# Softmax over rows of 512: one load of 32 rows in place of two of 16, and one reciprocal moved ahead of one maximum

## The chip, the cores and the metric

The kernel runs on one core of a Trainium2 chip. The core has several engines, each with its own stream of instructions. Three of them compute here: VectorE (DVE in the profile), ScalarE (ACT) and GpSimd (POOL). A fourth, SyncE (SP), only issues transfers between the chip's DRAM and the core's on-chip memory; the transfers themselves are carried by 16 DMA engines. TensorE is not used. Engines wait for one another through semaphores.

The metric is the time of one execution on the device in microseconds (us). Before the change it is 159.53 us, the median of three runs that lie between 159.28 and 159.63. A difference of less than 0.2% (0.32 us) can hardly be told from no change.

## The reference

```python
x: (16, 1024, 512) float32
x_max = np.max(x, axis=-1, keepdims=True)
exp_x = np.exp(x - x_max)
return exp_x / np.sum(exp_x, axis=-1, keepdims=True)
```

It is a softmax along the last axis of 16,384 rows of 512 numbers: 33.55 MB are read and 33.55 MB are written.

## The kernel before, in words

The 16,384 rows are spread over the 128 partitions of the on-chip memory, 128 rows to a partition, and below "row 40" means the 40th row of every partition. Rows are transferred in blocks and computed in groups of 8. So there are 16 groups: rows 0 to 7 are group 0, rows 32 to 39 are group 4, rows 120 to 127 are group 15.

**Transfers.** `BLOCKS` (line 21) cuts the 128 rows into blocks. Inside a block each partition's rows are neighbours in DRAM, so a block of 16 rows is one piece of 32 KB for each partition, and a block of 32 rows one of 64 KB (`in_dram`). `ORDER` (line 22) lists loads ("L") and stores ("S") in the order in which SP issues them. Before, it is: loads of rows 0-15, 16-31, 32-47, 48-63, 64-95; then stores of 0-15, 16-31, 32-47; loads of 96-111 and 112-127; stores of 48-63, 64-95, 96-111, 112-127. A store may take half of a block, and `in_dram` then takes half of each partition's piece. The first `AHEAD` entries are issued at once, without a wait; the very first load is even moved ahead of the program's opening barrier. Every later one waits for what it needs: a store for the groups that it holds, a load into the ring of 96 rows (`held`) for the store of the rows that lay there. `AFTER` (line 41) adds waits of a chosen kind: the first store is not issued before group 4 is scaled, the loads of 96 and 112 not before groups 8 and 9 are, and the store of 48-63 not before group 11 is.

All transfers go through one hardware queue, and each of the 16 DMA engines takes its share of them one after the other.

**Work on a group.** For group g:

- M*g*, on DVE (line 168): the negated maximum of each of its rows. DVE first waits for the load that holds the group (`take(nc.vector, loaded[k], 16)`).
- ACT (line 212), in a loop over the groups: for each row, the exponential with the maximum as bias, with its sum as a second result. It waits for M*g* once per group (`maxed`).
- P*g* (line 176, `scale`): DVE makes the reciprocal of the 8 sums, waiting for ACT's group g, and then POOL multiplies the rows by it (line 182). For groups 0 to 11.
- V*g*: the same with the multiplication on DVE. For groups 12 to 15.

DVE works through one list that is written out by hand, `VECTOR` (line 45). DVE takes it strictly in order: an entry that waits holds up all that are behind it. POOL takes its groups in order too, and each multiplication waits for its own reciprocal.

Of the kernel before, what the change touches and what calls it, by code (L numbers as in the profile page):

```python
# [17 lines left out]

BLOCKS = [(0, 16), (16, 32), (32, 48), (48, 64), (64, 96), (96, 112), (112, 128)]
ORDER = [
    ("L", (0, 16)),
    ("L", (16, 32)),
    ("L", (32, 48)),
    ("L", (48, 64)),
    ("L", (64, 96)),
    ("S", (0, 16)),
    ("S", (16, 32)),
# [5 lines left out]
    ("S", (96, 112)),  # L35
    ("S", (112, 128)),
]
AHEAD = 5

# [2 lines left out]


VECTOR = """
    M0 M1 P0 M2 P1 M3 P2 M4 P3 M5 P4 M6 P5 M7 P6 M8 P7 M9 P8 M10 P9 M11
    P10 P11 M12 M13 V12 M14 V13 M15 V14 V15
"""

# [24 lines left out]
def kernel(  # L75
# [13 lines left out]
    def in_dram(rows, a, b):  # L89

        first, last = next(k for k in BLOCKS if k[0] <= a and b <= k[1])
        block = rows[first * P : last * P].rearrange("(p r) d -> p r d", p=P)
# [34 lines left out]
    def load(k):  # L127
        copy = nc.sync.dma_start(out=rows(*k), in_=in_dram(x_rows, *k))
        copy.then_inc(loaded[k], 16)
        return copy  # L130
# [4 lines left out]
    with tc.manual_schedule():  # L135
        for _, k in ORDER[:AHEAD]:
            tc.no_tile_sem_insts.add(load(k).ins.name)
# [3 lines left out]
    taken, done = set(), set()  # L141
    for what, k in ORDER[AHEAD:]:
        for g in range(GROUPS):
# [112 lines left out]
```

## Time and profile before

| what | value |
|---|---|
| median of three runs | 159.53 us |
| the profiled execution's own time | 159.34 us |
| its span, first to last instruction | 158.0 us |
| DMA: 67.11 MB in 14 transfers | mean 425 GB/s |
| POOL, 12 multiplications | 83.7 us busy, 7018 ns each |
| DVE, 16 maxima | 70.2 us busy, 4398 ns each |
| ACT, 128 exponentials | 90.4 us busy, 707 ns each |
| DVE, 16 reciprocals | 3.2 us busy, 201 ns each |

The profile is of one execution; times in it are counted from the span's start. The 1.3 us between the span and the execution's own time lie before and after the instructions. "DVEq L112" and the like is an engine's queue that waits in `take` (line 112) for a semaphore. A DMA packet is what one DMA engine moves at a time: 32 KB (one partition's piece of 16 rows), 64 KB (of 32 rows), or the 4 bytes with which each engine reports at the end of a transfer; the transfer has landed when all 16 have reported.

From the trace's records, the five loads at the head landed in full at 12.28, 21.98, 31.68, 41.41 and 60.76 us.

### The profile page before, as it was taken

Reading aid. Unit: us, or ns where it says so; the run is one execution under the profiler, and the core shown is the slowest. Engines: PE = TensorE matmul, PEld = TensorE weight load, DVE = VectorE, ACT = ScalarE, POOL = GpSimd, SP = SyncE. Lnnn points to the kernel's source line nnn. Section 1 sums busy time; section 2 is a strip of 40 time slices with the busy share of each in tenths; the row PEclk is TensorE's granted clock in tenths of the full one; section 3 lists DMA queues with packets and bytes.
Section 4 is the critical chain, followed back from the end, with each engine's and each line's share of the span. In section 5 each row is a group of like instructions: output and inputs, shape, how many; then the busy total and the mean of one; then the engine's idle time right before and its main releaser. Section 6 shows DMA issues by size and latency. Waiting matters only on the chain. (4 is left out here: it accounts for less than half of the span.)

```text
span 158.0 us, 716 instructions
## 1 busy us (share of the span) xinstructions
DVE 90.0 (57%) x36; ACT 92.1 (58%) x257; POOL 83.9 (53%) x16
## 2 busy tenths in 40 slices
DVE  0008959778877915969770000695999996920000
ACT  1100699999999998399999300049946839000000
POOL 0000009999999999999999999991000000000000
DMA  8999999999969979999999999999999969999996
GB/s 265 423 481 423 398 456 465 406 415 481 564 265 531 481 315 398 423 481 423 398 448 465 406 406 398 415 498 415 398 448 481 531 265 531 390 406 406 465 456 265
DMA packets 2016, 67.11 MB, mean 425 GB/s; under 512 B 224, under 2 KB 224, under 8 KB 224
## 3 DMA queue, kind: packets, MB, share of 16 engines
q1 hardware_dynamic: 2016, 67.11, 99.1%
HBM read 33.55 MB, written 33.55 MB: 425 GB/s over the span
## 5 line engine op out<-in xcount | busy, mean ns | idle before, releaser
L212 ACT ACTIVATE held<-held,shift x128 | 90.4, 707 | 39.0 <-ACTq L112 39.0
L182 POOL TENSOR_TENSOR held<-held,recip 128x4096 f32<-128x4096 f32 x12 | 83.7, 7018 | 23.1 <-POOLq L112 23.1
L168 DVE TENSOR_REDUCE shift<-held 128x8 f32<-128x4096 f32 x16 | 70.2, 4398 | 27.7 <-DVEq L112 27.7
L212 ACT ACTIVATION_READ_ACCUMULATOR held<-held,shift x128 | 23.9, 187 | 0.0
L182 DVE TENSOR_TENSOR held<-held,recip 128x4096 f32<-128x4096 f32 x4 | 17.7, 4424 | 0.1
L176 DVE RECIPROCAL recip<-sums 128x8 f32<-128x8 f32 x16 | 3.2, 201 | 21.4 <-ACT held L212 19.5
L205 ACT ACT_TABLE_LOAD x1 | 1.3, 1283 | 3.4 <-PEq L139 3.4
L240 POOL MEMSET const-float32-0.0<- 128x1 f32 x1 | 0.1, 99 | 0.2 <-issue 0.2
L240 POOL MEMSET const-bfloat16-1.0<- 128x1 bf16 x1 | 0.1, 102 | 0.0
L240 POOL MEMSET const-uint8-127<- 128x1 uint8 x1 | 0.1, 102 | 0.0
L240 POOL MEMSET const-float32-1.0<- 128x1 f32 x1 | 0.1, 99 | 0.0
## 6 DMA issues: line engine op xcount, KB each, us to landing
held<-in_x_dram SPq DMA_DIRECT2D x6, 4096.0 KB, 18.7
out_dram<-held SPq DMA_DIRECT2D x6, 4096.0 KB, 19.8
held<-in_x_dram SPq DMA_DIRECT2D x1, 58.5
out_dram<-held SPq DMA_DIRECT2D x1, 30.8
```

The lines of the kernel that those rows point to most:

```text
L168: nc.vector.reduce_max(out=stats(shift, g), in_=rows(*group(g)), axis=AX, negate=True).then_inc(maxed, 1)
L176: ratio = nc.vector.reciprocal(out=stats(recip, g), in_=stats(sums, g))
L182: product = engine.tensor_mul(out=rows(*group(g)), in0=rows(*group(g)), in1=stats(recip, g).unsqueeze(2).to_broadcast([P, GROUP, d]),)
L205: nc.scalar.preload_act_table(EXP)
L212: act = nc.scalar.activation(out=row, in_=row, func=EXP, bias=shift[:, at], scale=1.0, accum_out=sums[:, at],)
L240: nc = _bacc.Bacc("TRN2", target_bir_lowering=False, num_devices=1)
```

## The change

The blocks (32, 48) and (48, 64) become one block (32, 64), and so do their two loads, which makes the loads at the head four instead of five. In DRAM the rows of the new block are dealt to the partitions 32 at a time, as in block (64, 96). The stores of rows 32-47 and 48-63 stay two transfers; each now takes half of every partition's 64 KB. On DVE, P3 goes ahead of M4.

```diff
-BLOCKS = [(0, 16), (16, 32), (32, 48), (48, 64), (64, 96), (96, 112), (112, 128)]
+BLOCKS = [(0, 16), (16, 32), (32, 64), (64, 96), (96, 112), (112, 128)]
 ORDER = [
     ("L", (0, 16)),
     ("L", (16, 32)),
-    ("L", (32, 48)),
-    ("L", (48, 64)),
+    ("L", (32, 64)),
     ("L", (64, 96)),
     ("S", (0, 16)),
...
-AHEAD = 5
+AHEAD = 4
...
 VECTOR = """
-    M0 M1 P0 M2 P1 M3 P2 M4 P3 M5 P4 M6 P5 M7 P6 M8 P7 M9 P8 M10 P9 M11
+    M0 M1 P0 M2 P1 M3 P2 P3 M4 M5 P4 M6 P5 M7 P6 M8 P7 M9 P8 M10 P9 M11
     P10 P11 M12 M13 V12 M14 V13 M15 V14 V15
 """
```

## The prediction

> **What bounds the kernel now.** First the page's parts on busy time and on DMA queues.
>
> ```profile
> DVE 90.0 (57%) x36; ACT 92.1 (58%) x257; POOL 83.9 (53%) x16
> q1 hardware_dynamic: 2016, 67.11, 99.1%
> ```
>
> No computing engine is busy for more than 58% of the span, and the one DMA queue keeps its 16 engines busy for 99.1%. So the time is the packets of 14 transfers end to end. Computing costs something only where a transfer is issued too late and the DMA engines run dry. The question is at which hand-over from one transfer to the next that is close. All loads at the head are queued by 2.65 us, so the first candidate is the first store: in the timelines of POOL and of SP,
>
> ```profile
> 51.45 13.99 POOL L182 TENSOR_TENSOR held<-held,recip 128x4096 f32<-128x4096 f32 x2
> 58.56 0.35 SPq L155 DMA_DIRECT2D out_dram<-held  x1
> ```
>
> POOL starts group 4 at 51.45 (the row holds groups 4 and 5) and ends it 7.02 later, at 58.46; SP issues the store 0.10 after that, at 58.56. How long an issue takes to become packets is seen in the DMA view of the first 2 us (40 slices of 0.05 us, counted by the packets' starts), and how close this hand-over is in the same view of 59.4 to 60.4 us (slices of 0.025 us):
>
> ```profile
> DMA  0000000000000000000099999999000000000000
> DMA packets 16, 0.52 MB, mean 262 GB/s; under 512 B 0, under 2 KB 0, under 8 KB 0
> ...
> DMA  0000000000090000090099990900900000999000
> DMA packets 32, 0.52 MB, mean 524 GB/s; under 512 B 16, under 2 KB 16, under 8 KB 16
> ```
>
> In the first, idle engines get their first packets in slices 20 to 27: by the records 1.02 to 1.39 us after the issue at 0.00. In the second, 16 engines report the end of the last load (4 bytes) and start on the store (32 KB) in the same slices, from 59.68 to 60.31 by the records: no gap at all, but the first engine starts on the store only 1.11 us after its issue. So there is hardly any slack here. The store of 48-63, issued at 107.38, is as close: there one engine stood idle for 0.15 us and got its first packet 1.56 us after the issue. The other hand-overs have 2.4 us or more.
>
> Third, DVE's timeline, which tells when maxima and reciprocals come:
>
> ```profile
> 28.74 4.37 DVE L168 TENSOR_REDUCE shift<-held 128x8 f32<-128x4096 f32 x1
> 34.27 0.20 DVE L176 RECIPROCAL recip<-sums 128x8 f32<-128x8 f32 x1 [1.16 <-ACT held L212]
> 34.39 4.42 DVE L168 TENSOR_REDUCE shift<-held 128x8 f32<-128x4096 f32 x1
> 39.91 0.20 DVE L176 RECIPROCAL recip<-sums 128x8 f32<-128x8 f32 x1 [1.10 <-ACT held L212]
> ...
> 45.55 0.20 DVE L176 RECIPROCAL recip<-sums 128x8 f32<-128x8 f32 x1 [1.16 <-ACT held L212]
> ...
> 51.20 0.20 DVE L176 RECIPROCAL recip<-sums 128x8 f32<-128x8 f32 x1 [1.11 <-ACT held L212]
> ...
> 60.89 4.42 DVE L168 TENSOR_REDUCE shift<-held 128x8 f32<-128x4096 f32 x1 [3.85 <-DVEq L112]
> ...
> 71.44 0.20 DVE L176 RECIPROCAL recip<-sums 128x8 f32<-128x8 f32 x1 [1.74 <-ACT held L212]
> ```
>
> and in ACT's
>
> ```profile
> 65.66 0.72 ACT L212 ACTIVATE held<-held,shift  x1 [3.20 <-ACTq L112]
> ```
>
> The rows at 34.39, 39.91 and 45.55 are M4, P3 and P4. M8 (60.89) is the pattern for a group that waits for its load: landed at 60.76, M8 0.13 later, ACT on group 8 at 65.66 (4.77 after M8's start), P8 at 71.44 (5.78 after that).
>
> **The change, part by part.**
>
> *One load for two.* By the landings, two loads of 16 rows took 19.43 us (21.98 to 41.41), and the one of 32 rows 19.34 (41.41 to 60.76). So the loads end 0.09 earlier: the last engine is free for the store at 60.22 instead of 60.31, the first at 59.59. Between no gain and this 0.09 I take the row itself. The issue that SP saves (0.4 to 0.5 us near 1.6) hides behind the first load.
>
> The Trainium skill prices a transfer higher: "DMA: Bandwidth & Descriptors", section "Anatomy of one DMA", fits about 2.0 us fixed plus the bytes' time for each. By that one transfer less would give about 157.5. The rows above, 0.09 for two against one, do not bear it out while a queue holds several.
>
> *Rows 32 to 47 land later.* They came at 31.68 and now come with the whole block, at 21.98 + 19.34 = 41.32. M4 moves from 34.39 to 41.32 + 0.13 = 41.46. ACT was fed without a break through groups 3, 4 and 5 (P3, P4, P5 are 5.65 apart); now it ends group 3 at 39.9 and starts group 4 at 41.46 + 4.77 = 46.22, so it idles for 6.3 us. P4 moves from 45.55 to 46.22 + 5.78 = 52.01. Adding 0.20 for the reciprocal and 0.04 until the waiting multiplication starts (the gap in the one place where POOL's queue waits for a reciprocal), POOL has group 4 at 52.25. Before, its reciprocal was 5.7 us early; POOL was free at 51.45. So POOL now waits, for 0.80 us, ends group 4 at 59.26, and SP issues the first store at 59.36.
>
> Behind P4 on DVE stand M6, P5 and so on. M6 starts at 52.13 and ends at 56.5, before ACT ends group 5 (57.5); P5 comes at 57.65, and POOL wants it at 59.23. P6 and later have more, since ACT's groups are 5.65 apart and POOL's 6.97. M8 would come at 63.4 instead of 60.89, behind P6, P8 at 74.6, POOL wants it at 80.1. So POOL's 0.80 neither grows nor shrinks to its end.
>
> *P3 ahead of M4.* P3 needs ACT's group 3 (39.9), and M4 now can't start before 41.46: P3 keeps its 39.91, and M4 loses nothing. Without the swap P3 would stand behind M4's wait until 45.8, over 1 us late for POOL's group 3 at 44.47. Cost nil.
>
> *The stores of 32-47 and 48-63* now write 32 KB of every 64 KB. No row shows this; the transfers of 64-95 put their pieces at the same distance and run at the usual pace (2.418 us per 64 KB packet against 1.213 per 32 KB), so I take nil. The slowest transfer of 32 KB packets in the records, the load of 96-111, took 0.46 us of packet time more than its like; twice that, 0.92, is the upper bound; none speaks for a gain.
>
> *The first store, late by 0.80.* Engines are free from 59.59 to 60.22. The store's packets come at 59.36 plus 1.02 to 1.39 by the head's rows, up to 1.56 by the one store that came late: the last at 60.76 to 60.93. Before, the last engine started on it at 60.31. So all that follows is late by 0.45 to 0.62. I take 0.62, the row of the same kind of transfer in the same place in the program. Whether a store's first packet into an empty engine is longer, as the head's loads are (1.53 to 2.28 against 1.21), isn't shown: the store's packet after 0.15 idle took 1.22. I take nothing, with up to 1.06 more as the other end.
>
> *Does it come twice?* The store of 48-63 waits for POOL's group 11, now 0.80 late: issued at 108.18, its last packets come by 109.74. The engines reach it at 109.27 + 0.62 = 109.89 at the latest. So the second lateness hides in the first. Nothing is close behind it: the next store is issued 0.46 later, the last two more than 8 us early.
>
> Sum: 159.34 + 0.62 = 159.96 on the profiled execution, which lies 0.19 under the median; on the median, 159.53 + 0.62 = 160.15.
>
> **The rivals.**
>
> *The store is there in time (not slower).* If a store is turned into packets within 60.22 - 59.36 = 0.86 us, the last engine doesn't wait, and only the 0.09 is left: 159.44, no change. For it: at 59.68 the first engine had its packet 1.11 after the issue without a gap, so the true time there is only known to be at most that. Against: 16 idle engines at the head all needed 1.02 or more. 10%, and most of it is a partial effect, about 0.2.
>
> The Trainium skill gives this its number: "DMA: Bandwidth & Descriptors", section "Specifications", has about 0.6 us to the first byte for transfers issued from SP. By that the packets would be there from 59.96 and the sum be 159.44; the head's 1.02 to 1.39 disagrees.
>
> *An empty queue costs more than the wait.* If the store's first packets are stretched as the first load's were (1.95 on the mean, 0.74 more), it is 160.89; with the slower halves of the stores, up to 161.8. For it: loads do it. Against: the 1.22 us packet, and that a store reads on-chip memory. 17%.
>
> *The load is split in effect, or merging saves more.* If M4 could start on the block's first half, at about 31.7, P4 would stay where it was and 159.44 be left; but `rowmax` waits for all 16 reports, which each engine sends behind its last packet. A gain over 0.32 would need a saving by the merge three times the 0.09 of the rows, and no wait after it. 4%.
>
> The fixed cost that the Trainium skill names (above) would be such a gain.
>
> **How the numbers follow.** The forecast holds 69%, no harm 10%, the stretched restart 17%, a gain 4%. Differences under 0.2% (0.32 us) can't be told from none, and the forecast's low end of 0.45 is near that, so some of it counts as the same: slower 0.80, same 0.16, faster 0.04. The range goes from 159.7 (a partial effect) to 160.9 (the stretched restart); the forecast's own is 159.95 to 160.3.
>
> **What would show it.** M4 at 41.5, P4 at 52.0, POOL idle 0.8 before group 4, the first store issued near 59.36; a gap of 0.2 to 1.3 us on every DMA engine near 60, and the last load's end 0.09 earlier; no larger gap at 109. Wrong would be: no gap near 60 (rival one), first store packets of 1.5 us or more (rival two), 32 KB packets longer than 1.22 in the stores of 32-63, or POOL waiting for P5 or later.

## The result, and the profile after

The changed kernel takes 160.06 us (median of 16 runs, 159.78 to 160.46) against 159.46 (16 runs, 159.23 to 159.79) before: the ratio is 1.0037, with a 95% interval of 1.0029 to 1.0045. That is 0.60 us slower, where 0.62 was forecast. The profiled execution of the changed kernel took 159.79, 0.45 more than the one of before, and its span is 158.5 instead of 158.0. It is a quick one among its runs, so the terms below are made against 0.45.

The page after, the same two rows:

```profile
DVE 90.1 (57%) x36; ACT 92.1 (58%) x257; POOL 84.0 (53%) x16
q1 hardware_dynamic: 1872, 67.11, 98.8%
```

The work is the same to 0.1 us. The DMA queue, which is the bound, is busy for 98.8% of a longer span instead of 99.1%. The timelines of DVE and ACT:

```profile
34.13 0.20 DVE L175 RECIPROCAL recip<-sums 128x8 f32<-128x8 f32 x1 [1.16 <-ACT held L211]
39.76 0.20 DVE L175 RECIPROCAL recip<-sums 128x8 f32<-128x8 f32 x1 [5.43 <-ACT held L211]
41.33 8.75 DVE L167 TENSOR_REDUCE shift<-held 128x8 f32<-128x4096 f32 x2 [1.36 <-DVEq L111]
51.87 0.20 DVE L175 RECIPROCAL recip<-sums 128x8 f32<-128x8 f32 x1 [1.80 <-ACT held L211]
51.99 4.37 DVE L167 TENSOR_REDUCE shift<-held 128x8 f32<-128x4096 f32 x1
57.51 0.20 DVE L175 RECIPROCAL recip<-sums 128x8 f32<-128x8 f32 x1 [1.16 <-ACT held L211]
```

```profile
46.09 0.72 ACT L211 ACTIVATE held<-held,shift  x1 [6.36 <-ACTq L111]
```

P3 (39.76) keeps its time, 0.15 earlier, as this execution's first load landed 0.14 earlier. M4 waits for the merged load and starts at 41.33, ACT idles for 6.36 us ahead of group 4, and P4 comes at 51.87. Then POOL, SP, and the DMA view of 59.4 to 60.4 us (slices of 0.025 us):

```profile
44.33 7.02 POOL L181 TENSOR_TENSOR held<-held,recip 128x4096 f32<-128x4096 f32 x1
52.16 7.02 POOL L181 TENSOR_TENSOR held<-held,recip 128x4096 f32<-128x4096 f32 x1 [0.81 <-DVE recip L175]
```

```profile
59.27 0.88 SPq L154 DMA_DIRECT2D out_dram<-held  x2
```

```profile
DMA  0000000000000000000000000000999999900000
DMA packets 32, 0.52 MB, mean 524 GB/s; under 512 B 16, under 2 KB 16, under 8 KB 16
```

POOL is idle for 0.81 us behind group 3, the first store is issued at 59.27, and no packet of it starts before slice 28; before, most engines had gone on to the store by then. By the records, the engines end the last load between 59.70 and 60.10 and start on the store between 60.12 and 60.27. On the mean they are idle for 0.29.

What the mean engine did from there on says where the 0.45 went (packet time and idle time per engine, from the trace's records, us):

| | before | after |
|---|---|---|
| loads at the head, end of the last one | 59.99 | 59.89 |
| idle ahead of the first store | 0.01 | 0.29 |
| stores of 0-15 and 16-31 | 19.43 | 19.55 |
| store of 32-47 and load of 96-111, with gaps | 19.94 | 20.07 |
| all that follows, to the last packet's end | 58.09 | 58.11 |

The head gives 0.10, half of it a slightly earlier first load; the idle time costs 0.28, the stores 0.12, the store and load behind them 0.13. The mean engine ends at 157.82 instead of 157.36, 0.46 later, which these terms make with 0.02 for the rest. (An engine's packets overlap by a few ns, so the columns add up to slightly more than the ends.)

### The profile page after: what moved, and what is told of

It reads as the page before. It is cut to its first block, busy times and chain, and to the rows that moved or that the text cites. A ratio compares the mean times of both kernels' runs of the same rounds, so it can differ in the third digit from the quotient of the medians.

```text
span 158.5 us, 714 instructions
## 1 busy us (share of the span) xinstructions
DVE 90.1 (57%) x36; ACT 92.1 (58%) x257; POOL 84.0 (53%) x16
## 3 DMA queue, kind: packets, MB, share of 16 engines
q1 hardware_dynamic: 1872, 67.11, 98.8%
```

## The experiments

All times are medians; the kernel before, run beside them, took 159.44 to 159.50.

**The swap alone.**

```diff
 # the kernel before
-M3 P2 M4 P3 M5 P4
+M3 P2 P3 M4 M5 P4
```

> The kernel before with the order on DVE alone changed (P3 ahead of M4). M4 then starts at 40.03 instead of 34.39, ACT's group 4 near 44.8, P4 near 50.6 instead of 45.6, and POOL wants it at 51.45, 0.7 us later than it would be there. Theory (the swap alone costs nothing): POOL without a gap, the first store at 58.56, 159.46, ratio 0.999 to 1.001. The rival, that the swap is a cost of its own: P4 later than 51.2, POOL idle, over 159.7.

159.46, ratio 1.0006 (0.9997 to 1.0015): no change. In the timelines of DVE and POOL of this kernel

```profile
50.47 0.20 DVE L176 RECIPROCAL recip<-sums 128x8 f32<-128x8 f32 x1 [1.80 <-ACT held L212]
```

```profile
37.38 69.78 POOL L182 TENSOR_TENSOR held<-held,recip 128x4096 f32<-128x4096 f32 x10
```

P4 is at 50.47, five us later than before, and POOL runs through ten groups without a gap. P4 had room, and the swap uses most of it without a cost.

**The rows' new place alone.**

```diff
 # the kernel before, ORDER, AHEAD and VECTOR as they were
-BLOCKS = [..., (32, 48), (48, 64), (64, 96), ...]
+BLOCKS = [..., (32, 64), (64, 96), ...]
```

> The kernel before with the changed rows' place in DRAM alone: the block 32-63 is dealt 32 rows to a partition, but still loaded by two transfers of 16 rows, with the old order on DVE. Loads and stores of 32-47 and 48-63 then all move 32 KB of every 64 KB. Theory 1 (the place costs nothing): 159.46, ratio 0.999 to 1.001, packets of these four transfers at 1.213 to 1.222 us. Theory 2 (half pieces are dearer): 159.65 to 159.9, with packets of 1.24 to 1.26 us in the store of 32-47.

159.47, ratio 1.0002 (0.9993 to 1.0011). Loads of half pieces run at 1.213 us a packet, the store of 32-47 at 1.227 on the mean against 1.221 before. The place costs nothing that can be measured.

**The merged load without the swap.**

```diff
 # the changed kernel
-M3 P2 P3 M4 M5 P4
+M3 P2 M4 P3 M5 P4
```

> The changed kernel with the old order on VectorE: P3 behind M4. P3 then waits for the load of 32-63 with M4 and comes near 45.7, POOL's group 3 starts near 45.95 instead of 44.33 and group 4 near 52.9 instead of 52.16. The first store is issued near 60.05, 0.77 later than in the changed kernel. Theory (each us by which that store is later is a us of the time once the engines have run dry): 160.06 + 0.77 = 160.8. If the swap did nothing: 160.06.

160.78, ratio 1.0080 (1.0067 to 1.0093), 0.72 over the changed kernel. POOL's and SP's timelines:

```profile
46.05 13.99 POOL L181 TENSOR_TENSOR held<-held,recip 128x4096 f32<-128x4096 f32 x2 [1.56 <-DVE recip L175]
```

```profile
60.14 0.88 SPq L154 DMA_DIRECT2D out_dram<-held  x2
```

POOL loses 1.56 at group 3, the store is issued 0.87 later than with the swap, and the engines are idle for 1.06 on the mean. So with the merged load the swap is worth 0.7 us; it doesn't repair P4.

**P4 late, and nothing else.** The kernel before, with its two loads; on DVE M6 and a maximum of six rows of zeros, of which nobody uses the result, go ahead of P4.

```diff
-M4 P3 M5 P4 M6 P5 M7
+M4 P3 M5 M6 G6 P4 P5 M7
...
+    def delay(n):          # G6: n = 6
+        nc.vector.reduce_max(out=spent[:, :n],
+            in_=blank.unsqueeze(1).to_broadcast([P, n, d]), axis=AX)
```

> The kernel before, with its two loads of 16 rows, and on VectorE a maximum of six rows that nobody uses ahead of P4 (and M6 ahead of that), so that P4 comes at 52.05 instead of 45.55 and POOL's group 4 at 52.27, as late as in the changed kernel. Theory (P4's lateness and nothing else in the change costs time): POOL idle 0.8, the first store issued near 59.35, the DMA engines idle by 0.2 to 0.3, and the time of the changed kernel, 160.0 to 160.2. Rival (the merged load or the places of its rows carry part of it): between 159.5 and 159.9.

160.12, ratio 1.0042 (1.0029 to 1.0055): the time of the changed kernel. POOL's timeline, SP's, and the DMA view of 59.4 to 60.4 us:

```profile
52.09 7.02 POOL L192 TENSOR_TENSOR held<-held,recip 128x4096 f32<-128x4096 f32 x1 [0.69 <-DVE recip L186]
```

```profile
59.20 0.88 SPq L157 DMA_DIRECT2D out_dram<-held  x2
```

```profile
DMA  0000000000000000000000000099999909000000
```

It is nearly the same picture, without the merged load; POOL is idle for 0.69 instead of 0.81. The engines' idle time is 0.19 on the mean, the two stores take 19.54 and the store and load behind them 20.14: the terms of the table above come with it, and the mean engine ends 0.48 later than in the kernel before.

The time itself says less than it seems to. The span from the first to the last instruction is 0.46 longer than in the kernel before (means of 5 and 11 runs); another 0.25 is lost outside the span, where this kernel spends 1.58 us and the kernel before 1.34. The changed kernel spends 1.32 there, so its loss of 0.6 lies inside. Why the kernel with the added operation takes longer outside its span was not looked into. So P4's lateness is shown to make most of the loss, 0.46 of 0.6 with a lateness that is 0.1 smaller. That it makes all of it fits these runs, but their noise doesn't decide it.

**The first store 7 us late.** The kernel before, to measure what a late issue costs at this hand-over.

```diff
-AFTER = {("S", 0): 4, ...
+AFTER = {("S", 0): 5, ...
```

> The kernel before, but the first store waits for group 5, which POOL ends at 65.44: issued at 65.53, 6.97 later, with all DMA engines idle for over 6 us. This measures how long an issued store takes to become packets and whether its first packets are longer after a gap. If it takes 0.84 to 1.00 us as in the profile after: first packets at 66.4 to 66.5, on the mean 6.45 later than before, time 165.8 to 166.0. If it takes the head's 1.02 to 1.39: 166.1 to 166.4. If the packets behind a gap are dearer by the 0.010 us of the store in the profile after (1.224 against 1.214), 0.09 us more for this store. If a first packet is stretched like the head's loads, 0.7 more.

167.18, ratio 1.0482 (1.0467 to 1.0498). SP's timeline, and the DMA view of 65 to 67 us (slices of 0.05):

```profile
65.63 0.35 SPq L155 DMA_DIRECT2D out_dram<-held  x1
```

```profile
DMA  0000000000000000000000000000099990000000
```

The idle engines start on the store 0.85 to 0.99 us after its issue; the changed kernel has 0.84 to 1.00 and the run before this one 0.85 to 1.00 (one engine there starts at 1.03, straight from the last load). Its first packets take 1.23 to 1.24, not the 1.5 to 2.3 of the head's loads. The later packets of that store take 1.224 against 1.214, also as in the changed kernel, and the two stores 19.55. So behind an idle stretch the first two stores lose 0.12, however long the stretch was. The time is 1.2 to 1.4 over what this latency gave in the expectation: the last load, of 112-127, took 10.48 instead of 9.70 and the store and load of 32-47 and 96-111 took 20.43 instead of 19.94. The next transfers had been queued 9 us ahead of their turn here, which the next two runs take up.

**The first store much earlier.** In the changed kernel (first) and in the kernel before (second):

```diff
-AFTER = {("S", 0): 4, ...
+AFTER = {("S", 0): 3, ...
```

> The changed kernel, but the first store waits for group 3 instead of group 4, so that SP issues it near 51.5 us, long before the loads at the head end near 59.9. Theory 1 (the loss is the hand-over at 60 us alone: group 4 scaled 0.8 late, the store issued at 59.27 instead of 58.56, the DMA engines idle 0.29 us on the mean): no idle time at 60, and the loss is gone: 159.46 - 0.09 = 159.37, ratio to before 0.999 to 1.000. Theory 2 (the hand-over is about half of it, since the profiles differ by 0.29 - 0.10 there, and the stores with half pieces and the transfers behind them make the rest): 159.65 to 159.85, and the store of 32-47 stays at 10.0 us instead of 9.77.

> The kernel before, but the first store waits for group 3 instead of 4 and is issued near 51.5. Theory A (a transfer of the other direction that is queued long before the one in flight ends makes the last packets of that one longer, as in the run with the changed kernel and this edit, where packets that started 3 us before the switch took 0.74 us more for each engine): the last load's packets longer again, 159.45 + 0.74 = 160.2, with no gap. Theory B (that loss belongs to the merged load or to the stores of half pieces): 159.45 and the last load at 19.35.

160.39, ratio 1.0077 (1.0053 to 1.0101), and 160.25, ratio 1.0042 (1.0028 to 1.0056). Both theories of the first fell; the second run was made to find out why, and its theory A held. The stretch from the start of the last load to its end, in the kernel before and in the changed kernel with the early store (columns: stretch, its length, busy times, clock, DMA share, GB/s):

```profile
40.66:59.99 19.33, 12.96 (x6) 19.33 (x55) 19.33 (x4) 1.00 0.96 417
```

```profile
40.65:60.71 20.06, 16.41 (x6) 14.61 (x41) 19.24 (x4) 1.00 0.98 408
```

And of the kernel before with the early store, SP's and DVE's timelines:

```profile
51.48 0.82 SPq L155 DMA_DIRECT2D out_dram<-held  x2
```

```profile
61.78 4.42 DVE L168 TENSOR_REDUCE shift<-held 128x8 f32<-128x4096 f32 x1 [4.86 <-DVEq L112]
```

The stores sit in the queue from 51.5 on, no engine is idle, and yet the last load is slower: M8 starts at 61.78 instead of 60.89. By the records the packets that started between 57 and 58 us, the last of this load on each engine, took on the mean 0.74 (first) and 1.01 us (second) more than others of their size, and hardly any other packet of the load did. A store queued 1.1 us ahead of the switch, as before, costs nothing of the kind. `AFTER`'s wait for group 4 is thus worth 0.7 to 0.8 us, and issuing the store much earlier is no cure.

**The first store in time, by another gate.** The changed kernel, and the kernel with P4 late alone. The first store now waits for a small DVE operation:

```diff
-M6 P5 M7            (changed kernel)
+M6 P5 G1 M7
-M7 P6 M8            (P4 late alone)
+M7 P6 G2 M8
...
-AFTER = {("S", 0): 4, ...
+AFTER = {...
...
+        if (what, k[0]) in GATE:       # SP, ahead of the first store
+            take(nc.sync, gates[what, k[0]], 1)
...
+    delay(n).then_inc(gates[...], 1)   # DVE
```

> The changed kernel, but the first store waits for a small VectorE operation behind P5 (a maximum of one row, written nowhere that counts) instead of POOL's group 4, and so is issued near 58.35, 1.3 to 1.8 us before the engines end the last load. POOL's group 4 stays 0.8 late. Theory (what costs is when the first store is issued, and nothing else in the change): no gap, no longer packets, 159.45 - 0.09 = 159.35 to 159.5. Rival (POOL's lateness itself, or the half pieces, cost time further on): 159.7 or more.

> The kernel before with its two loads, P4 made late as in the run of that alone, and the first store taken off POOL: it waits for a maximum of two rows behind P6 and is issued near 58.2, in time. So this is the run of the changed kernel with the first gate (160.99), without the merged load. Theory A (that run lost its time because POOL, 0.8 late, issues the load of 96-111 and the store of 48-63 late, at 87.2 and 108.05, while the DMA engines are now not late): the same here, idle time near 89 and 109, 160.5 to 161.1. Theory B (that loss belongs to the merged load or the rows' new place): 159.45 to 159.6.

160.99, ratio 1.0097 (1.0074 to 1.0119), and 160.54, ratio 1.0059 (1.0037 to 1.0080). The gate did what it should: issue at 58.51 and 58.52, no gap at 60. The time still went up. SP's timeline and the DMA view of 108.4 to 110.4 us (slices of 0.05), of the changed kernel with the gate and then of P4 late with the gate:

```profile
108.22 0.82 SPq L161 DMA_DIRECT2D out_dram<-held  x2
```

```profile
DMA  9000000000000999990999099000000000000999
```

```profile
108.41 0.82 SPq L162 DMA_DIRECT2D out_dram<-held  x2
```

```profile
DMA  0090000000000000099990090999000000000000
```

POOL is still 0.7 to 0.8 late, so the store of 48-63 is issued 0.8 or more after the time of before, while the DMA engines come to it no later than in the changed kernel: they are idle for 0.16 and 0.21 on the mean. The load of 96-111 is late too (87.37 and 87.55), and it and the store ahead of it take 20.35 and 20.17 instead of 19.94. So the theory of the first of these two runs, that nothing but the first store's issue costs, fell. Of the second, theory A held for the idle time at 109; near 89 it is 0.03 on the mean. The late first store had hidden the later ones.

Of the 0.9 to 1.0 us that the second run loses, 0.42 lie outside the span (1.74 against 1.32) and 0.53 inside, as much as with P4 late alone. So without the merged load, taking away the first lateness gained nothing. The first run spends only 1.32 outside the span and loses 1.5 inside. The records show where the difference lies: in both the mean engine ends at 158.0, but in the first one engine starts on the load of 96-111 at 90.53, 3.2 us after its issue and 1.5 after it had ended the store, and it ends 1.1 behind the mean (the last engine of the other run 0.3). Why that engine started so late stays open.

**More gates.** Two gates in the changed kernel (a second one, G3 behind P10, ahead of the load of 96-111), three (G1 ahead of P10 for that load, G5 behind M12 for the store of 48-63, and the entries of `AFTER` for these two dropped), and in the kernel before one alone, G4 behind P10 in place of entry 8:

```diff
 # two gates
-P10 P11
+P10 G3 P11
 # three gates
-P9 M11 P10 P11 M12 M13
+P9 M11 G1 P10 P11 M12 G5 M13
 # the kernel before
-P10 P11
+P10 G4 P11
```

> The gate of the run before, and a second one of the same kind (a maximum of three rows behind P10) for the load of 96-111, which then is issued near 87.7 instead of 87.2, some 1.3 to 1.9 us before the engines end the store of 32-47. Before, that load was issued 2.4 to 3.0 us ahead, and store and load together took 0.5 us longer than their like. Theory A: that half microsecond shrinks as well, 158.9 to 159.2, faster than both kernels. Theory B (the switch from stores to loads costs this whatever the time of the issue): as with the first gate alone, 159.35 to 159.5.

> The changed kernel, with all three hand-overs between loads and stores taken off POOL's late chain: small VectorE operations, of which nobody uses the result, let SP issue the first store near 58.35, the load of 96-111 near 85.3 and the store of 48-63 near 107.3. Group 4 stays 0.8 late on POOL. Theory (the lateness acts through these three issues alone; with the first store's gate alone it came out again at the load of 96-111 and at the store of 48-63): 159.37 or less; if the load of 96-111, now 3.4 to 4.0 ahead of its turn, costs no longer packets, as in the run of before with the store after group 3 (lead 3.3 to 3.9, none), 158.9. Rival (gates of this kind cost time themselves, or the changed kernel has another loss): 159.8 or more.

> The kernel before, but the load of 96-111 waits for a small VectorE operation behind P10 instead of POOL's group 8 and is issued near 85.25 instead of 86.53, that is 3.7 to 4.3 us ahead of its turn instead of 2.4 to 3.0. Theory A (there is a lead at which the switch from store to load costs nothing, as seen once at 3.3 to 3.9): the 0.5 us that store and load took more than their like is gone, 158.95, ratio 0.997. Theory B (a lead over 3 us costs 0.74 there as it does at the first store): 159.7. Theory C (no dependence): 159.46.

160.12 (1.0043, 1.0029 to 1.0058), 160.77 (1.0077, 1.0061 to 1.0092) and 160.18 (1.0059, 1.0036 to 1.0082). Only one fits any of its theories: with three gates the rival, 159.8 or more. All three lose time outside the span too, 0.29, 0.37 and 0.26; inside it they lose 0.36, 0.95 and 0.63. Inside the span two gates thus lose less than the changed kernel's 0.6, but the time doesn't gain by it. With two gates the load is issued at 87.68, 1.0 us ahead of its turn, and store and load still take 20.23. With three, that load landed so late that M12 came at 101.62 and the gate behind it let the store of 48-63 go only at 108.87: the run says nothing on its theory. In the kernel before with an earlier load, store and load take 20.0 on the mean, as before, and the mean engine ends at the same 157.36; but the engines' ends, 0.62 apart before, are 1.11 apart, and the last one ends 0.49 later.

How the cost of the switch from store to load depends on the lead, the time from a transfer's issue to its turn on the first engine, stays open. Over the 19.41 of two such transfers at the normal pace, it was 0.82 at a lead of 1.0 us (two gates), 0.94 and 0.75 at 1.3 (one gate), 0.21 at 2.2 and 0.02 at 3.3 (the early first stores), 0.53 to 0.73 at 2.3 to 2.5 (the kernel before, the changed one, P4 late alone), 1.30 at 3.7 (three gates), 0.59 at 4.0 and 1.02 at 9.6: no rule, and lead isn't all that differs between these runs. No version was found that beats the kernel before.

## Why the prediction was right, and where its steps were not

**The bound and the place.** Right: the DMA queue is the bound, the first store's hand-over is where it breaks, and P4 is why.

**One load for two.** By the landings 19.34 (21.85 to 41.19), as forecast, against 19.43. On the mean engine the gain is 0.04.

**Rows 32 to 47 later.** Right step by step: ACT's group 4 at 46.09 (46.22 forecast), P4 at 51.87 (52.01), POOL's idle time 0.81 (0.80), the store at 59.27 (59.36); they differ by 0.09 to 0.14, about what the first load of this execution was earlier, and the idle time by 0.01. P5 and later kept their room.

**P3 ahead of M4, and the stores' half pieces.** Nil each, as the runs of each alone show; without the swap 0.72 more. One sign that was to show the prediction wrong did come: the packets of the store of 32-47 take 1.255 on the mean, against 1.221 before. With half pieces alone they take 1.227, and with P4 late alone, without half pieces, 1.253; so it comes with the lateness and not with the half pieces.

**The first store, late by 0.80.** This step failed, though the sum came out; that 0.62 met the measured 0.60 is luck. It took the last engine's start on the store, at 59.36 plus 1.39 to 1.56, as what delays everything, by 0.45 to 0.62. The store needs only 0.84 to 1.00 from issue to packet, so the last engine started on it at 60.27, 0.04 earlier than the 60.31 of before, and the store even landed at the same 70.47. By the step's own rule that is no loss at all. Nor was there the gap of 0.2 us or more that was forecast for every engine: it was 0.01 to 0.57, and next to nothing on the engines that ended the load last. The head's row, 1.02 to 1.39, was of another moment, and the 1.56 of the one late engine was not the general case. What the step missed is that the other engines, which had gone on to the store up to 0.6 ahead of the last one, lost that head start: 0.28 on the mean. And it took packets behind a gap as unchanged, where two stores lost 0.12, and the store and load at the next switch, from stores to loads, 0.13. In landings the loss appears only there: 0.07 at the store of 16-31, 0.25 at that of 32-47, 0.36 at the load of 96-111. That the engines' spread had absorbed part of that switch's cost before fits this, but wasn't tested.

The Trainium skill, "DMA: Bandwidth & Descriptors", section "Specifications", gives about 0.6 us to the first byte. From the issue's start the runs show 0.84 to 1.00, and from its end, 0.35 later, 0.50 to 0.65. So the page agrees if it is counted from the issue's end. Counted from its start, as in the prediction, its 0.6 is some 0.3 below the mean of 0.91, and the head's row, 1.18 on the mean, some 0.3 above it.

**Does it come twice?** Right for the changed kernel: the gap at 109 is 0.03 on the mean against 0.02 before. The runs with gates show how it hides: with the first lateness taken away, the later ones cost as much (0.53 inside the span against 0.46, without the merged load).

**The rivals.** The store in time: its condition, packets within 0.86 us, was met for some engines and missed by 0.14 at most for others, and yet the kernel was slower; the condition was put on the wrong engine. The stretched restart: fell, first packets take 1.23. A larger gain by the merge: fell, the head gains 0.04 on the mean engine. The fit of the Trainium skill that the prediction sets beside it ("DMA: Bandwidth & Descriptors", section "Anatomy of one DMA") is stated there for transfers issued from GpSimd, and these are issued from SP.

## What to carry to other kernels

Where the DMA queue is the bound, a merged load is paid for at its first row: half of what it brings lands as late as the rest, and the question is which store, far down the chain, is issued just in time by the group that now comes late. Follow the lateness to every issue that hangs on the same engine, since repairing the first only uncovers the next. Reckon with the mean of the DMA engines as well as with the last: the others' head start is a reserve, and a gap uses it up without a trace in the next landing. And when an operation is added to a kernel to test a cause, compare the spans as well as the times, since it can cost time outside the span.

## What the runs showed of the hardware

- A store queued 9 us ahead of the switch from loads made the last packet of the load ahead, on each engine, 0.74 and 1.01 us longer on the mean (two kernels); queued 1.1 to 1.3 us ahead, it cost nothing of the kind. For the switch from stores to loads the runs give no rule.
- When the loads had run out, a store's packets started on the idle engines 0.84 to 1.00 us after SP's issue in four runs. This is not a bound: with the first gate in the changed kernel, one engine that had been idle for 1.5 us got its first packet of the load of 96-111 3.2 us after the issue.
- Behind an idle stretch of 0.2 to 6.5 us, the engines start within 0.2 us of one another instead of 0.6, and the first store's later packets take 1.224 instead of 1.214 us.
- Five of the six kernels with added DVE operations spend 1.58 to 1.74 us outside the span of their instructions, against 1.31 to 1.34 for the kernel before beside them; the sixth, the changed kernel with the first gate alone, spends 1.32. The cause is open.
